# A two-layer decoder trunk: where the planes of h's second block lie, which raw buffer comes when, and where the FFN's combining stands

## The chip, the cores and the metric

The kernel runs on one core of a Trainium2 chip. The metric is the time of one execution on the device in microseconds (us), lower is better. Engines are named as in the profile: PE multiplies matrices, ACT (ScalarE) and DVE (VectorE) work on elements, POOL is GpSimd, and SP issues nearly all DMAs, in the order of its queue.

## The reference

Two layers over a residual stream of 256 tokens and 2048 features, in float32. Each layer normalises, runs a mixer (layer 0: window attention beside an mLSTM; layer 1: forgetting attention), projects its output and adds it to the stream; then it normalises again and runs a SwiGLU FFN with 5632 hidden features. A final norm follows. The FFN, around whose start the change lies:

```python
h = rms_norm(x, norm_ffn)
x = x + (silu(h @ w_gate) * (h @ w_up)) @ w_down
```

## The kernel before

**Products.** Every float32 operand is split into a high part (fp32r, a cast on ACT) and a low part (the difference, on DVE). A product of two operands is three matmuls: high x high, high x low, low x high (L244 to L246 in `gemm`, L557 to L559 in `three`). Weights arrive raw from DRAM, 256 rows x 512 columns (512 KB) at a time, by `load_raw` (L145, queue SP); L206 and L380 are casts, L207 and L381 the differences. A split weight lies in a slot of the pool `wp` (six of them, tag `hi`) or, in the FFN, in one of five such slots (`stock`) or two `triples` (tiles hi0/lo0 and hi1/lo1, 512 columns x 3).

**The FFN.** 11 groups of 512 hidden features per layer for gate and up, in three parts (`PARTS`), each part followed by two down groups. A group is one call of `pair_group`: it walks the 16 row blocks of the activation in eight pairs, in the order of a table. Kind 0 is a plain pair: its two weights are split by L206/L207 and take eight block products of three matmuls. Kind 1 is a *mixed* pair, here also *seven-product pair*: seven such products instead of eight, with weights that are sums and differences of raw blocks (L645, L648, L649 on DVE, done in the raw buffer, then L380/L381).

```python
ORDER = ((0, 0), (1, 1), (0, 2), (1, 3), (0, 4), (1, 5), (0, 6), (0, 7))
```

A mixed pair's raw weights (gate's half, then up's) go to one of three buffers taken in turn (`quads`): two tiles of the FFN's pool with the tag `quad`, and `own`, a slot of `wp`, which the projection ahead of the FFN still uses. The four mixed products (`prods`) of a group add up over its mixed pairs. `combine` merges them into the tile `c` (one buffer): a copy on ACT (L577) and three additions on DVE (L579 to L581). Then the plain sums are added (L696), silu and the gate follow (L698, L700), and the result is turned by DMA for the down groups (L729, L731, joined L736).

**The planes of h.** The projection ahead of the FFN (`out_proj`) finishes the stream h in four blocks n = 0 to 3 of 512 features. Each is turned for use as the FFN's left operand: ACT copies its halves to planes (L338), SP issues four DMA transposes (L340), and later a step called join copies the turned planes together (L345) and splits them into xh and xl (L386 on ACT, L387 on DVE, sums L326 and L294 to L297). `scrap` says where a block's planes lie meanwhile: n = 0 and 2 in the tile `c`, n = 3 in the tiles sd0/sd1, n = 1 in a quad buffer. Pairs 0 and 1 of a group need block 0, pairs 2 and 3 block 1, 4 and 5 block 2, 6 and 7 block 3.

**What sets the order.** The code emits instructions in program order; a scheduler then orders each engine's instructions by its own estimate of when their inputs and buffers are ready, earlier emitted first. So both a buffer and the place of emission move instructions on every engine.

Of the kernel before, what the change touches and what calls it, by code (L numbers as in the profile page):

```python
# [7 lines left out]
F32 = mybir.dt.float32  # L8
BF16 = mybir.dt.bfloat16
F32R = mybir.dt.float32r  # L10
# [7 lines left out]
P = 128  # L18
# [5 lines left out]
NB = 512  # L24
CK = 2
# [29 lines left out]
QUADS = 2  # L55
# [20 lines left out]
def trunk(  # L76
# [27 lines left out]
    stock, triples, quads = [], [], []  # L104
# [262 lines left out]
    def scrap(fp, n):  # L367
        if n % 2 == 0:
            box = fp.tile([P, 4, NB], F32, tag="c", name="box", bufs=1)
            halves = box[:, 0:2, :], box[:, 2:4, :]  # L370
        elif n == 3:
            halves = [fp.tile([P, 3, NB], F32, tag=f"sd{i}", name="box", bufs=1)[:, 0:CK, :] for i in range(2)]
        else:
            box = fp.tile([P, 2 * CK, NB], F32, tag="quad", name="box", bufs=QUADS)
            halves = box[:, 0:2, :], box[:, 2:4, :]
        flat, turned = (a.rearrange("p a n -> p (a n)") for a in halves)
        return flat, turned.bitcast(U16).rearrange("p (b k t q) -> p b k t q", b=2, t=NT, q=P)

# [182 lines left out]
    def pair_group(fp, par, lhs, sums, mats, order, todo=(), halves=None, inner=None, raws=None):  # L561
        plain = [two_banks(par, "acc") for _ in range(2)]
        begun = set()

        def fresh(*at):
            known = at in begun
            begun.add(at)
            return not known

        todo = list(todo)  # L570
        prods = None
        kinds = [kind for kind, _ in order]
        t0, t1 = slice(0, P), slice(P, 2 * P)

        def combine(prods):
            c = fp.tile([P, 4, NB], F32, tag="c", name="c", bufs=1)
            nc.scalar.copy(c[:, 0, :], prods[0])  # L577
            if halves is None:
                nc.vector.tensor_tensor(out=c[:, 1, :], in0=prods[3], in1=c[:, 0, :], op=ALU.add)  # L579
                nc.vector.tensor_tensor(out=c[:, 2, :], in0=prods[2], in1=c[:, 1, :], op=ALU.add)  # L580
                nc.vector.tensor_tensor(  # L581
                    out=c[:, 1:4:2, :],
                    in0=prods[1].rearrange("p (a n) -> p a n", a=1).broadcast_to([P, 2, NB]),
                    in1=c[:, 1:3, :],
                    op=ALU.add,
                )
                return c
            nc.vector.tensor_tensor(out=c[:, 2, :], in0=prods[3], in1=c[:, 0, :], op=ALU.add)
            nc.vector.tensor_tensor(out=c[:, 1, :], in0=prods[2], in1=c[:, 2, :], op=ALU.add)
            nc.vector.tensor_tensor(out=c[:, 3, :], in0=prods[1], in1=c[:, 1, :], op=ALU.add)  # L590
            nc.vector.tensor_tensor(out=c[:, 2, :], in0=prods[1], in1=c[:, 2, :], op=ALU.add)
            return c

        for pos, (kind, pair) in enumerate(order):
            k0 = 2 * pair
            if inner is not None and pos == len(order) - 1:
                c = combine(prods)
                inner()
            if not kind:
                last = pos == len(order) - 1  # L600
                walk = [(i, t) for i in range(CK) for t in range(NT)]
                if last:
                    walk.sort(key=lambda it: it[1])
                for m, (w, c0) in enumerate(mats):
                    hi, lo = load_chunk(w, k0, c0, NB)
                    run_due(todo, pos)
                    for i, t in walk:
                        ah, al = lhs(k0 + i)
                        ts = slice(t * P, (t + 1) * P)
                        three(  # L610
                            plain[m][t], ah[:, ts], al[:, ts], hi[:, i, :], lo[:, i, :],
                            fresh(m, t), last and i == CK - 1,
                        )
                continue
            first, last = 1 not in kinds[:pos], 1 not in kinds[pos + 1 :]
            if first:
                if 1 - par and halves:
                    prods = [pm.tile([P, NB], F32, tag="pm", name="prod") for _ in range(4)]
                else:
                    prods = two_banks(1 - par, "prod") + two_banks(1 - par, "prod")  # L620
            if halves:
                ra, rb = (load_raw(w, k0, c0, NB, fp, W_RAWS, raws) for w, c0 in mats)
                hg, lg = split_chunk(ra, NB)
                run_due(todo, pos)
                hu, lu = (m[:, 0, :] for m in slot())
                split_plain(hu, lu, rb[:, 0, :])
                nc.vector.tensor_tensor(out=ra[:, 1, :], in0=rb[:, 1, :], in1=ra[:, 1, :], op=ALU.subtract)
                nc.vector.tensor_tensor(out=rb[:, 1, :], in0=rb[:, 1, :], in1=rb[:, 0, :], op=ALU.subtract)
                nc.vector.tensor_tensor(out=rb[:, 0, :], in0=rb[:, 0, :], in1=ra[:, 1, :], op=ALU.subtract)
                nc.vector.tensor_tensor(out=ra[:, 0, :], in0=ra[:, 0, :], in1=rb[:, 0, :], op=ALU.subtract)  # L630
                parts = []
                for src in (ra, rb):
                    hs, ls = halves.pop(0)
                    halves.append((hs, ls))
                    split_plain(hs, ls, src)
                    parts += [(hs[:, b, :], ls[:, b, :]) for b in range(CK)]
            else:
                raw = quad()
                for m, (w, c0) in enumerate(mats):
                    load_raw(w, k0, c0, NB, into=raw[:, CK * m : CK * (m + 1), :])  # L640
                hg, lg = triple()
                latest[0] = split_plain(hg, lg, raw[:, 0:3, :])
                hu, lu = hg[:, 2, :], lg[:, 2, :]
                run_due(todo, pos)
                nc.vector.tensor_tensor(  # L645
                    out=raw[:, 1:4:2, :], in0=raw[:, 3:4, :].broadcast_to([P, 2, NB]), in1=raw[:, 1:3, :], op=ALU.subtract
                )
                nc.vector.tensor_tensor(out=raw[:, 2, :], in0=raw[:, 2, :], in1=raw[:, 1, :], op=ALU.subtract)  # L648
                nc.vector.tensor_tensor(out=raw[:, 0, :], in0=raw[:, 0, :], in1=raw[:, 2, :], op=ALU.subtract)  # L649
                (h1, l1), (h0, l0) = slot(), slot()  # L650
                split_plain(h1, l1, raw[:, 1:4:2, :])
                split_plain(h0, l0, raw[:, 0:3:2, :])
                parts = [((h0, h1)[b % 2][:, b // 2, :], (l0, l1)[b % 2][:, b // 2, :]) for b in range(4)]
            sh, sl = sums(pair)
            xa, la = lhs(k0)
            xb, lb = lhs(k0 + 1)
            three(prods[0], xb[:, t0], lb[:, t0], hg[:, 1, :], lg[:, 1, :], first, last)
            three(plain[0][0], xa[:, t0], la[:, t0], hg[:, 0, :], lg[:, 0, :], fresh(0, 0), False)
            three(plain[1][0], sh[3], sl[3], hu, lu, fresh(1, 0), False)
            three(prods[1], sh[0], sl[0], *parts[1], first, last)  # L660
            three(prods[2], sh[2], sl[2], *parts[3], first, last)
            three(prods[3], sh[1], sl[1], *parts[2], first, last)
            three(plain[0][1], xa[:, t1], la[:, t1], *parts[0], fresh(0, 1), False)
        if inner is None:
            c = combine(prods)
        return plain, c

# [128 lines left out]
    def close_layer(layer, w_out, idx, key, **rest):  # L796
        with tc.tile_pool(name=f"fp{layer}", bufs=2) as fp:
# [4 lines left out]
            x4 = fp.tile([P, 2, P], F32R, name="x4", bufs=1)  # L802
            todo = out_proj(w_out, idx, key, (*sx, x4, fp))
            sd = [fp.tile([P, nd, 4, P], F32R, tag=f"sd{i}", name=f"sd{i}", bufs=1) for i in range(2)]
            triples.extend([fp.tile([P, 3, NB], F32R, name=f"{a}{i}", bufs=1) for a in ("hi", "lo")] for i in range(2))
            stock.extend([slot() for _ in range(5)])
            own = wp.tile([P, 2, CK, NB], F32R, tag="hi", name="raw").rearrange("p a k n -> p (a k) n").bitcast(F32)
            quads.extend(fp.tile([P, 2 * CK, NB], F32, tag="quad", name="raw", bufs=QUADS) for _ in range(QUADS))
            quads.insert(1, own)
            ffn(layer, fp, sx, x4, sd, key, todo, **rest)  # L810
            stock.clear()
            triples.clear()
# [4 lines left out]
    hi, lo = slot()  # L817
# [17 lines left out]
    with tc.tile_pool(name="ev", bufs=1) as ev:  # L835
# [225 lines left out]
        with tc.tile_pool(name="mp", bufs=1) as mp:  # L1061
# [8 lines left out]
            halves = spare_halves()  # L1070
# [11 lines left out]
            c = pair_even(OFF_QM, OFF_KM, MIXQ, [(G3_AT, gates_3)])  # L1082
# [111 lines left out]
    with tc.tile_pool(name="od", bufs=1) as od:  # L1194
# [70 lines left out]
        halves = spare_halves()  # L1265
# [152 lines left out]
```

## Time and profile before

| | |
|---|---|
| median of 3 runs | 2090.94 us (2088.95 to 2092.37) |
| profiled execution | 2090.14 us |
| its span, first to last instruction | 2088.4 us |
| granted TensorE clock, mean | 0.998 |
| PE / DVE / ACT / POOL busy | 2071.4 / 1806.3 / 1367.1 / 44.0 us |
| DMA queue of SP, share of 16 engines | 65.1% |

A row of a timeline gives start (us from the span's start), duration, engine, line, operation, the tile written and those read, the shape, and in square brackets the idle time ahead of it with what ended it. A row of a table by stretches gives the stretch, its length, the busy time of PE, PEld, DVE, ACT and POOL with the count of instructions (x), the granted clock, the DMA engines' share and GB/s. A row of a group gives busy time, mean ns of one, and the idle time before them. Steps of layer 0's FFN begin near 300 us, those of layer 1's near 1365 us.

### The profile page before, as it was taken

What the parts mean: (1) busy time and instruction counts of PE and PEld (TensorE: products, weight loads), DVE (VectorE), ACT (ScalarE), POOL (GpSimd) and SP (SyncE); (2) the same over time, 40 slices, a digit from 0 to 9 for tenths busy, and PEclk for the clock granted to TensorE, in tenths of its full rate; (3) what the DMA queues carried; (4) which work ended last, traced back from release to release, by engine and by line L of the source; (5) the groups of instructions that cost most, each with busy time, mean ns of one, the idle gap of its engine ahead of it and who ended that gap; (6) DMA issues with size and microseconds to landing.
All of it is one profiled execution on the core that took longest, in us unless ns stands there. A gap on an engine that the chain in (4) does not pass through costs nothing.

```text
span 2088.4 us, 26470 instructions
## 1 busy us (share of the span) xinstructions
PE 2071.4 (99%) x9473; PEld 1714.7 (82%) x9473; DVE 1806.3 (86%) x2169; ACT 1367.1 (65%) x1649; POOL 44.0 (2%) x69
## 2 busy tenths in 40 slices
PE   9999999999999999999999999999999999999998
PEld 7878887888888888888888888877888888888887
DVE  6788768989999989998899688679989999999984
ACT  6777677665577646667677676587655667556763
POOL 1010000000000000000000001000000000000000
PEclk9999999999999999999999999999999999999999
DMA  8566577765677666665676776585756766666754
GB/s 292 174 207 194 188 242 215 222 200 198 205 221 224 210 194 224 217 209 184 203 202 218 225 200 185 155 269 188 250 188 196 233 196 217 226 205 200 235 158 159
DMA packets 309572, 434.84 MB, mean 208 GB/s; under 512 B 106413, under 2 KB 114625, under 8 KB 309313
## 3 DMA queue, kind: packets, MB, share of 16 engines
q1 hardware_dynamic: 307088, 426.27, 65.1%
q0 software_dynamic: 1632, 5.80, 0.9%
q8 instruction: 74, 1.21, 0.2%
q10 hardware_dynamic: 720, 1.09, 0.2%
q14 instruction: 58, 0.47, 0.1%
HBM read 408.68 MB, written 2.12 MB: 197 GB/s over the span
## 4 chain that ended last, share of the span: by engine, by line
PE 89%; ACT 4%; DVE 3%; DMA 2%; issue 2%; SPq 0%; POOL 0%; POOLq 0%; ACTq 0%; DVEq 0%
PE acc L558 20%; PE acc L559 20%; PE acc L557 20%; PE prod L558 5%; PE prod L557 5%; PE prod L559 5%; PE acc L245 4%; PE acc L244 4%; PE acc L246 4%; DVE hi L207 1%; ACT box L345 1%; PE p L411 1%; ACT hi L206 1%; ACT hi L380 1%; DMA raw<-in_w_gate_dram 1%
## 5 line engine op out<-in xcount | busy, mean ns | idle before, releaser
L206 ACT CAST hi<-raw 128x1024 fp32r<-128x1024 f32 (+3 forms) x561 | 567.1, 1023 | 366.5 <-PE acc L559 179.4
L207 DVE TENSOR_TENSOR hi<-raw,hi 128x1024 fp32r<-128x1024 f32 (+3 forms) x561 | 657.9, 1186 | 137.2 <-ACT hi L206 134.7
L559 PE MATMUL acc<-hi,xl 128*128 128x512 f32 x1320 | 511.9, 389 | 0.0
L557 PE MATMUL acc<-hi,xh 128*128 128x512 f32 x1320 | 495.9, 390 | 0.8 <-ACT xh L386 0.6
L380 ACT CAST hi<-raw 128x1024 fp32r<-128x1024 f32 (+2 forms) x299 | 344.9, 1168 | 225.8 <-PE acc L559 192.7
L558 PE MATMUL acc<-hi,xh 128*128 128x512 f32 x1254 | 488.0, 390 | 0.2 <-DVE hi L207 0.2
L557 PEld LDWEIGHTS acc<-hi,xh 128*128 128x128 f32 x1320 | 247.6, 188 | 53.5 <-ACT xh L386 1.8
L559 PEld LDWEIGHTS acc<-hi,xl 128*128 128x128 f32 x1320 | 248.0, 188 | 51.5
L558 PEld LDWEIGHTS acc<-hi,xh 128*128 128x128 f32 x1254 | 235.4, 188 | 50.0 <-DVE hi L207 1.0
L381 DVE TENSOR_TENSOR hi<-raw,hi 128x1024 fp32r<-128x1024 f32 (+1 forms) x204 | 240.2, 1180 | 11.1 <-ACT hi L380 10.4
L381 DVE TENSOR_TENSOR lo<-raw,hi 128x1536 fp32r<-128x1536 f32 x95 | 166.6, 1754 | 43.6 <-ACT hi L380 40.0
L559 PE MATMUL acc<-hi,ml 128*128 128x512 f32 x466 | 181.0, 389 | 0.0
L557 PE MATMUL acc<-hi,mh 128*128 128x512 f32 x466 | 173.3, 389 | 0.0
L558 PE MATMUL acc<-hi,mh 128*128 128x512 f32 x437 | 170.3, 390 | 0.4 <-DVE hi L207 0.4
L245 PE MATMUL acc<-hi,mh 128*128 128x512 f32 (+1 forms) x322 | 126.3, 392 | 0.0
L244 PE MATMUL acc<-hi,mh 128*128 128x512 f32 (+1 forms) x322 | 125.8, 391 | 0.0
L246 PE MATMUL acc<-hi,ml 128*128 128x512 f32 (+1 forms) x322 | 123.7, 391 | 0.0
L645 DVE TENSOR_TENSOR raw<-raw 128x1024 f32<-128x1024 f32 x95 | 115.5, 1217 | 0.4
L557 PEld LDWEIGHTS acc<-hi,mh 128*128 128x128 f32 x466 | 87.5, 188 | 18.6 <-ACT hi L206 0.4
L559 PEld LDWEIGHTS acc<-hi,ml 128*128 128x128 f32 x466 | 87.5, 188 | 18.1
L245 PE MATMUL acc<-hi,xh 128*128 128x512 f32 (+3 forms) x288 | 99.8, 347 | 0.2 <-DVE hi L207 0.2
L246 PE MATMUL acc<-hi,xl 128*128 128x512 f32 (+3 forms) x288 | 99.1, 345 | 0.0
(364 smaller groups left out, 3073.9 us busy)
## 6 DMA issues: line engine op xcount, KB each, us to landing
raw<-in_w_gate_dram SPq DMA_DIRECT2D x176, 512.0 KB, 4.3
raw<-in_w_up_dram SPq DMA_DIRECT2D x176, 512.0 KB, 4.8
raw<-in_w_down_dram SPq DMA_DIRECT2D x176, 512.0 KB, 4.8
raw<-in_w_in_odd_dram SPq DMA_DIRECT2D x88, 512.0 KB, 5.2
raw<-in_w_in_even_dram SPq DMA_DIRECT2D x51, 512.0 KB, 5.0
raw<-in_w_out_even_dram SPq DMA_DIRECT2D x32, 512.0 KB, 5.3
raw<-in_w_out_odd_dram SPq DMA_DIRECT2D x32, 512.0 KB, 4.7
hr<-in_w_in_even_dram SPq DMA_DIRECT2D x12, 512.0 KB, 4.4
```

The source lines that it names most:

```text
L206: latest[0] = nc.scalar.copy(hi[:, k, 0:n], raw[:, k, 0:n])
L207: nc.vector.tensor_tensor(out=lo[:, k, 0:n], in0=raw[:, k, 0:n], in1=hi[:, k, 0:n].bitcast(F32), op=ALU.subtract)
L244: nc.tensor.matmul(o, ah[:, ts], hi, start=(k == 0), stop=False)
L245: nc.tensor.matmul(o, ah[:, ts], lo, start=False, stop=False)
L246: nc.tensor.matmul(o, al[:, ts], hi, start=False, stop=(k == k_all - 1 and cs.stop == n))
L345: nc.scalar.copy(ju[:, :, b], turned[:, b, :, :, :].rearrange("p k t q -> p (k t q)"))
L380: cast = nc.scalar.copy(dst_h, src)
L381: nc.vector.tensor_tensor(out=dst_l, in0=src, in1=dst_h.bitcast(F32), op=ALU.subtract)
L557: nc.tensor.matmul(o, ah, hi, start=start, stop=False)
L558: nc.tensor.matmul(o, ah, lo, start=False, stop=False)
L559: nc.tensor.matmul(o, al, hi, start=False, stop=stop)
L645: nc.vector.tensor_tensor(out=raw[:, 1:4:2, :], in0=raw[:, 3:4, :].broadcast_to([P, 2, NB]), in1=raw[:, 1:3, :], op=ALU.subtract)
```

## The change

Three edits; each engine executes as many instructions as before.

1. The planes of block n = 1 lie in the tiles hi1/lo1, the second triple, and not in a quad buffer. The triples get explicit tags for that.
2. In gate/up and down groups (`halves is None`) `combine` is emitted right behind the last mixed pair of the table, ahead of the plain pairs that follow it, and not at the group's end.
3. `own` is the third of the three raw buffers, not the second.

```diff
@@ scrap @@
         else:
-            box = fp.tile([P, 2 * CK, NB], F32, tag="quad", name="box", bufs=QUADS)
-            halves = box[:, 0:2, :], box[:, 2:4, :]
+            halves = [fp.tile([P, 3, NB], F32, tag=f"{a}1", name="box", bufs=1)[:, 0:CK, :] for a in ("hi", "lo")]
@@ pair_group @@
         for pos, (kind, pair) in enumerate(order):
             k0 = 2 * pair
+            if 1 not in kinds[pos:] and 1 in kinds[pos - 1 : pos] and halves is None:
+                c = combine(prods)
...
-        if inner is None:
+        if inner is None and halves is not None:
             c = combine(prods)
@@ close_layer @@
-            triples.extend([fp.tile([P, 3, NB], F32R, name=f"{a}{i}", bufs=1) for a in ("hi", "lo")] for i in range(2))
+            triples.extend([fp.tile([P, 3, NB], F32R, tag=f"{a}{i}", name=f"{a}{i}", bufs=1) for a in ("hi", "lo")] for i in range(2))
...
-            quads.insert(1, own)
+            quads.append(own)
```

Lines from L375 to L595 are one lower in the changed kernel (L380 is L379, L577 is L576, L579 is L578), later ones one higher (L645 is L646).

The queue of SP, layer 0, from the end of out_proj into the FFN, before. Here raw_2993 is the first mixed pair's buffer, raw_2992 is `own` with the second pair, raw_2994 holds the third; box_2922 are the planes of block 2, box_2970 those of block 3:

```order
L145 DMA raw_2869<-in_w_out_even_dram 128x2x512
L145 DMA raw_2993<-in_w_gate_dram 128x2x512
L145 DMA raw_2993<-in_w_up_dram 128x2x512
...
L145 DMA raw_2994<-in_w_gate_dram 128x2x512
L145 DMA raw_2994<-in_w_up_dram 128x2x512
...
L340 DMA_TRANSPOSE box_2922<-box_2922 128x4x128 x4
L145 DMA raw_2992<-in_w_gate_dram 128x2x512
L340 DMA_TRANSPOSE box_2970<-box_2969 128x4x128 x4
L145 DMA raw_2992<-in_w_up_dram 128x2x512
```

The same queue in the changed kernel, where raw_2994 is the first mixed pair's buffer, raw_2995 the second's and raw_2993 (`own`) the third's; box_2579 and box_2647 are blocks 0 and 1, box_2923 and box_2970 blocks 2 and 3:

```order
L145 DMA raw_2994<-in_w_gate_dram 128x2x512
...
L145 DMA raw_2994<-in_w_up_dram 128x2x512
...
L145 DMA raw_2995<-in_w_gate_dram 128x2x512
L145 DMA raw_2995<-in_w_up_dram 128x2x512
...
L340 DMA_TRANSPOSE box_2579<-box_2579 128x4x128 x4
L340 DMA_TRANSPOSE box_2648<-box_2647 128x4x128 x4
L145 DMA raw_2782<-in_w_out_even_dram 128x2x512
...
L340 DMA_TRANSPOSE box_2923<-box_2923 128x4x128 x4
L340 DMA_TRANSPOSE box_2971<-box_2970 128x4x128 x4
L145 DMA raw_2993<-in_w_gate_dram 128x2x512
L145 DMA raw_2993<-in_w_up_dram 128x2x512
```

The first two mixed pairs' loads have moved ahead of the transposes of blocks 0 and 1, the loads into `own` behind those of blocks 2 and 3, and the chunk raw_2782 of out_proj, which stood ahead of the eight transposes of blocks 0 and 1, stands behind them.

ACT at the start of layer 0's FFN, before (hi1_2985 is the second mixed pair's split out of `own`):

```order
L206 CAST hi_2987<-raw_3088 128x1024
L380 CAST hi0_2983<-raw_2994 128x1536
L345 COPY box_2969<-box_2970 128x1024 x2
L206 CAST hi_2990<-raw_3156 128x1024
L380 CAST hi1_2985<-raw_2992 128x1536
L345 COPY box_2922<-box_2922 128x1024 x2
L386 ACTIVATE xh_58<-box_2969,gT_93 128x256 x4
L206 CAST hi_2991<-raw_3172 128x1024
L386 ACTIVATE xh_58<-box_2922,gT_93 128x256 x4
```

The same place in the changed kernel:

```order
L206 CAST hi_2988<-raw_3089 128x1024
L345 COPY box_2923<-box_2923 128x1024 x2
L379 CAST hi_2989<-raw_2995 128x1024
L385 ACTIVATE xh_58<-box_2923,gT_93 128x256 x4
L326 ACTIVATE full_3119<-box_2923,gT_93 128x256 x2
L379 CAST hi_2990<-raw_2995 128x1024
L206 CAST hi_2991<-raw_3157 128x1024
L379 CAST hi0_2984<-raw_2993 128x1536
L345 COPY box_2970<-box_2971 128x1024 x2
```

Block 2 is joined ahead of block 3, the second mixed pair's first cast is gone from here (it stands ahead, in out_proj), and what is cast from `own` is the third pair.

DVE where the second gate/up group of layer 0 combines, before (raw_3627 and raw_3643 are already the next group's first plain pair, prod_3366 is a mixed sum):

```order
L645 TENSOR_TENSOR raw_2992<-raw_2992 128x2x512
L207 TENSOR_TENSOR hi_2989<-raw_3627,hi_2989 128x1024
L207 TENSOR_TENSOR hi_2990<-raw_3643,hi_2990 128x1024
L381 TENSOR_TENSOR sd1_2982<-s4_3535,sd0_2981 128x512
L648 TENSOR_TENSOR raw_2992<-raw_2992 128x512
L579 TENSOR_TENSOR c_3602<-prod_3366,c_3602 128x512
```

The same place in the changed kernel, where those weights are raw_3628 and raw_3644 and the sum is prod_3367:

```order
L207 TENSOR_TENSOR hi_2990<-raw_3628,hi_2990 128x1024
L646 TENSOR_TENSOR raw_2995<-raw_2995 128x2x512
L578 TENSOR_TENSOR c_3528<-prod_3367,c_3528 128x512
L380 TENSOR_TENSOR sd1_2983<-s4_3541,sd0_2982 128x512
L207 TENSOR_TENSOR hi_2991<-raw_3644,hi_2991 128x1024
L649 TENSOR_TENSOR raw_2995<-raw_2995 128x512
```

The first addition of the combining has moved ahead of one split of the next group, one smaller difference and one step of the next mixed pair's weights. It stands behind the splits of its own group's last plain pairs in both.

## The prediction

> **What bounds the kernel now.** I read the page's parts 1 and 2 first, then the busy time by stretches of 20 us, then TensorE's list of waits, and last the timeline of the places where PE loses.
>
> ```profile
> span 2088.4 us, 26470 instructions
> PE 2071.4 (99%) x9473; PEld 1714.7 (82%) x9473; DVE 1806.3 (86%) x2169; ACT 1367.1 (65%) x1649; POOL 44.0 (2%) x69
> ```
>
> PE is the bound almost throughout, so an edit that moves other engines' work gains only where PE waits. The table by stretches says where (the number behind PE's busy time counts matmuls):
>
> ```profile
> 280.00:300.00 20.00, 20.00 (x90) 16.54 (x90) 10.75 (x16) 16.47 (x25) 0.00 (x0) 1.00 0.72 206
> ...
> 340.00:360.00 20.00, 16.37 (x61) 11.91 (x62) 19.82 (x27) 18.61 (x26) 0.00 (x0) 0.91 0.48 157
> 360.00:380.00 20.00, 20.00 (x90) 16.56 (x89) 20.00 (x27) 12.16 (x13) 0.00 (x0) 1.00 0.75 256
> 380.00:400.00 20.00, 20.00 (x90) 16.54 (x89) 19.38 (x21) 15.94 (x17) 0.00 (x0) 1.00 0.62 183
> 400.00:420.00 20.00, 20.00 (x90) 16.57 (x89) 19.86 (x24) 10.71 (x12) 0.00 (x0) 1.00 0.86 290
> 480.00:500.00 20.00, 19.77 (x87) 16.25 (x87) 19.48 (x21) 6.78 (x7) 0.00 (x0) 1.00 0.76 260
> 1540.00:1560.00 20.00, 19.83 (x86) 15.99 (x86) 19.84 (x23) 7.22 (x8) 0.00 (x0) 1.00 0.77 262
> ```
>
> A full stretch has 90 matmuls, 20/90 = 0.222 us each. Two stretches, drawn around the losses, show what is missing at the head of each layer's FFN:
>
> ```profile
> 338.90:355.60 16.70, 12.21 (x44) 8.28 (x43) 15.64 (x23) 16.29 (x23) 0.00 (x0) 0.90 0.43 148
> 1404.00:1424.00 20.00, 17.99 (x71) 12.38 (x70) 19.41 (x30) 17.85 (x27) 0.00 (x0) 1.00 0.45 142
> ```
>
> Layer 0: 44 x 0.222 = 9.8 us of work in 16.7 us, 6.9 us lost. Layer 1: 71 x 0.222 = 15.8 us in 20, 4.2 us lost. The down groups' first stretches (x87, x86) lack 3 and 4 matmuls, 0.7 and 0.9 us. That is 12.7 us in all, and the bound of any gain here. The waits in layer 0, on the timelines of PE, ACT and SP:
>
> ```profile
> 341.17 0.50 PE L557 MATMUL prod<-hi,xh 128*128 128x512 f32 x1 [2.03 <-ACT hi L380]
> ...
> 342.96 0.80 PE L558 MATMUL prod<-lo,xh 128*128 128x512 f32 x1 [0.83 <-DVE lo L381]
> ...
> 346.53 0.50 PE L557 MATMUL acc<-hi,xh 128*128 128x512 f32 x1 [0.64 <-ACT xh L386]
> ...
> 355.40 0.50 PE L558 MATMUL prod<-hi,sx 128*128 128x512 f32 x1 [0.99 <-DVE hi L381]
> ```
>
> ```profile
> 336.28 2.56 ACT L345 COPY box<-box 128x1024 uint16<-128x1024 uint16 x2 [3.99 <-DMA box<-box]
> ...
> 339.64 1.47 ACT L380 CAST hi<-raw 128x1536 fp32r<-128x1536 f32 x1
> 341.01 2.55 ACT L345 COPY box<-box 128x1024 uint16<-128x1024 uint16 x2
> 343.43 1.70 ACT L386 ACTIVATE xh<-box,gT 128x256 fp32r<-128x256 f32 x4
> ```
>
> ```profile
> 329.18 0.53 SPq L145 DMA_DIRECT2D raw<-in_w_gate_dram  x1
> 329.80 5.14 SPq L340 DMA_TRANSPOSE box<-box  x4
> 335.00 0.58 SPq L145 DMA_DIRECT2D raw<-in_w_up_dram  x1
> ```
>
> The second seven-product pair's weights go to `own`, a slot of the wp pool that out-proj keeps until 329.18; their second half is issued at 335.00, behind the four transposes of block n=3; the cast of it (L380, 339.64) stands on ACT behind that block's join, and PE stops for it until 341.17. Next it lacks the lows (342.96), then block n=2's planes, joined at 341.01 only (346.53).
>
> **The change, part by part.** I name lines as in the kernel before.
>
> *Buffers (edits one and three).* With `own` as the third quad, pairs one and two both have quad buffers that are free early, since n=1's planes now lie in the second triple. In the order all four of their loads stand before the transposes of n=0 and n=1; pair two is cast and split during out-proj, and `own` takes pair three, behind the transposes of n=2 and n=3. On ACT the join of n=2 comes ahead of that of n=3. Nothing is added: each engine has as many instructions as before. What leaves 340 to 360 is pair two's splitting, by these groups:
>
> ```profile
> L381 DVE TENSOR_TENSOR lo<-raw,hi 128x1536 fp32r<-128x1536 f32 x95 | 166.6, 1754 | 43.6 <-ACT hi L380 40.0
> ...
> L645 DVE TENSOR_TENSOR raw<-raw 128x1024 f32<-128x1024 f32 x95 | 115.5, 1217 | 0.4
> ...
> L381 DVE TENSOR_TENSOR hi<-raw,hi 128x1024 fp32r<-128x1024 f32 (+1 forms) x204 | 240.2, 1180 | 11.1 <-ACT hi L380 10.4
> ...
> L649 DVE TENSOR_TENSOR raw<-raw 128x512 f32<-128x512 f32 x95 | 64.8, 682 | 0.1
> L648 DVE TENSOR_TENSOR raw<-raw 128x512 f32<-128x512 f32 x95 | 64.7, 682 | 0.2
> ```
>
> On DVE that is 1.75 + 1.22 + 0.68 + 0.68 + 2 x 1.18 = 6.7 us. The part that goes to 280 to 300, where DVE is busy 10.75 of 20 us, is hidden by idle time there. Without that cover the 6.7 us would come back as lateness in out-proj.
>
> Layer 0's first pause: its cast is done some 40 us early, so 2.03 + 0.83 us go, and with them the slow matmuls that follow (clock below). n=2's last transposes stand before the gate load of 329.18, so its join can run from about 331 on ACT; 2.56 us of join and 1.70 us of L386 bring its planes by about 335 to 336, and the 0.64 us at 346.53 goes too. Pair three's second half is issued at about 335.6 and lands some 5 us later (before, the half issued at 335.00 was being cast at 339.64), so its cast is done by about 342. In the new order PE reaches that pair 45 matmuls behind the place of the pause (338.97 + 45 x 0.227 = 349.2). Neither takes the pause's place.
>
> The limit is DVE. From 340 to 420 it is busy 19.82 + 20.00 + 19.38 + 19.86 = 79.1 us of 80. Take 6.7 us out; PE running 6.9 us earlier pulls as much later work in: 79.3 us of 80. It just fits on average, not at every instruction: walking the new order through these durations, the pieces of pair three come up to 1.4 us late around 352 to 356. I leave 1.4 us, a gain of 5.5 us; the ends are 3 us (half of the loss returns later) and 6.9.
>
> Layer 1 loses in smaller pieces, the largest of them here:
>
> ```profile
> 1397.71 1.48 ACT L380 CAST hi<-raw 128x1536 fp32r<-128x1536 f32 x1 [2.31 <-DMA raw<-in_w_up_dram]
> ...
> 1406.66 0.50 PE L557 MATMUL prod<-hi,xh 128*128 128x512 f32 x1 [0.69 <-ACT xh L386]
> 1410.94 0.72 PE L557 MATMUL prod<-hi,sx 128*128 128x512 f32 x2 [0.66 <-ACT hi L380]
> 1420.00:1440.00 20.00, 20.00 (x89) 16.12 (x88) 20.00 (x26) 12.00 (x13) 0.00 (x0) 1.00 0.76 259
> ```
>
> The 2.31 us of idle ACT and the 1.48 us cast behind it go, so the joins that follow start up to 3.8 us earlier and both pauses shrink. But DVE is busy all 20 us of the next stretch, and in my walk one split near 1431 comes some 1.7 us late. I take a gain of 2.0 of the 4.2 us, with ends at 0 and 4.2.
>
> *One queue pays.* One out-proj chunk, raw_2782 and its counterpart in layer 1, is now issued behind the eight transposes of n=0 and n=1. The place it takes is that of the chunk behind them before:
>
> ```profile
> 296.27 1.05 ACT L206 CAST hi<-raw 128x1024 fp32r<-128x1024 f32 x1 [1.89 <-DMA raw<-in_w_out_even_dram]
> 297.35 1.23 DVE L207 TENSOR_TENSOR hi<-raw,hi 128x1024 fp32r<-128x1024 f32 x1 [2.87 <-ACT hi L206]
> 299.54 0.39 PE L244 MATMUL acc<-hi,mh 128*128 128x512 f32 x1
> ```
>
> Its lows would be there at 298.6; PE wants them at about 299.5. The margin is 0.9 us, and not smaller in layer 1. I book nothing, with +2 us per layer as the worse end (a transfer that lands some 3 us late) and no gain possible, since PE runs without a gap there.
>
> *The combining.* In the order of gate/up groups its first DVE instruction (L579) moves ahead of one split L207 (of the next group's first pair), one L648 and one L381, and no further: `c` is a single tile, held until the group before has been joined from it.
>
> ```profile
> 407.66 2.35 DVE L207 TENSOR_TENSOR hi<-raw,hi 128x1024 fp32r<-128x1024 f32 x2
> ...
> 413.80 0.39 PE L558 MATMUL acc<-hi,xh 128*128 128x512 f32 x1
> ...
> L581 DVE TENSOR_TENSOR c<-prod,c 128x1024 f32<-128x1024 f32 x33 | 40.0, 1214 | 0.0
> ...
> L579 DVE TENSOR_TENSOR c<-prod,c 128x512 f32<-128x512 f32 x33 | 22.5, 681 | 1.8 <-PE prod L559 1.8
> ```
>
> PE at 413.80 reads what the first of the two splits wrote, which was done at 407.66 + 1.22 = 408.88: a lead of 4.9 us, one typical for the body. A delay of 0.68 us, even of the whole combining (0.68, as much for L580, and 1.21: 2.6 us), stays below that. A gain cannot come of it either where all 90 matmuls of a stretch are there already. I take 0, with ends at -1.6 us (the down groups' two starts) and +8 us (the rival below).
>
> The sum: -5.5 - 2.0 + 0 + 0 = -7.5 us. The profiled run took 2090.14 us, 1.7 us of it outside the span; it lies 0.8 us below the median, so 2082.6 on its scale is 2083.4 against the median; I say 2083.5.
>
> *The clock.* Layer 0's pauses were followed by a low clock; layer 1's, none above 0.7 us of idle PE, by none:
>
> ```profile
> 343.00:346.50 3.50, 2.89 (x6) 0.53 0.32 123
> ```
>
> At 0.53 for 3.5 us this costs about 1.6 us, already inside the 6.9. No stop of that length should be left, so the sum has no term for it; if the late chunk of out-proj stopped PE for 2 us, as the pause at 341 did, 1.6 us would come on top. [...]
>
> **The rivals.**
>
> *No change (0.22).* DVE becomes the bound: 79.3 of 80 us is an average, and if the work pulled in queues behind pair three's lows, PE stops at 352 and again up to 380 for what it gained. For it: DVE at 20.00 from 360 to 380. Against it: PE waits nowhere there now, with the same DVE share. Layer 0 then keeps a gain of 3 us and layer 1 none: 2090.9 - 3 = 2088.
>
> *Slower (0.18): the combining ahead of splits.* L577 on ACT and L579 on DVE now stand ahead of a split that PE needs next, and both wait for PE's last product of the seven-product pairs. An engine that gets there before PE has finished stands, and the splits queued behind it with it. It decides where that wait, the combining and the split itself pass the lead of 4.9 us: with 1.8 us, the one wait that L579's row has now, 1.8 + 2.6 + 1.2 = 5.6, 0.7 us too late. In each of the 22 gate/up groups (11 per layer) that is +15 us, less 7.5 at the heads: 2098.5; in half of them, 2091. Against it: L579 waits once in 33 now, and in the order it has passed one split only.
>
> *The change does not do what it says (0.02).* For the loads the order excludes it. For the combining it nearly holds, and then the time is the forecast's.
>
> **How the numbers follow.** The forecast (0.58) covers 2079 to 2086.5: all 11.1 us of the heads gone, or 4.5 us only. No change covers 2087 to 2092. The range of 2079 to 2095 takes in both and the part of the slower rival that strikes some groups only, or two late chunks (+3.6 us each) with the heads' gain lost. A measurement of this kernel tells 0.2%, 4.2 us, from no change. Faster by more than that: the forecast with a little of the second case, 0.60; slower by more: 0.18; within: 0.22.
>
> **What would show it.** Right: 338.9 to 355.6 with some 69 matmuls instead of 44 and no clock below 1.00; the L380 cast of pair two before 300; 1404 to 1424 with 80 or more; all stretches of 20 us from 360 on still at 90. Wrong: TensorE's waits showing L246 or L245 behind L206 near 299 (the late chunk); new waits of L558 on DVE L207 or L381 in every group, and L579's wait on PE grown from 1.8 us to tens of us (the slower rival); or waits of the old size, moved from 341 to 352 and later (no change).

## The result, and the profile after

The changed kernel takes 2082.85 us in the median (2082.55 to 2084.5, 6 runs), the kernel before 2091.88 us (2088.95 to 2093.99, 6 runs). The medians lie 9.0 us apart. The ratio is 0.9959, with a 95% interval of 0.9949 to 0.9969, which is 6.5 to 10.7 us less and clear of the 0.2% that could be told from no change.

The page of the changed kernel, its span and its engines:

```profile
span 2080.8 us, 26492 instructions
PE 2068.0 (99%) x9473; PEld 1715.3 (82%) x9473; DVE 1806.2 (87%) x2169; ACT 1368.0 (66%) x1649; POOL 43.2 (2%) x69
```

DVE, ACT and POOL are as busy as before to 1 us. PE stands 4.2 us less (span less busy time: 17.0 us before, 12.8 now), and its busy time fell by 3.4 us for the same 9473 matmuls. The old losses had both: from 338.9 to 355.6 PE stood, and was also booked busy for 12.21 us with 44 matmuls that take 9.8 at 0.222 us each. The table by stretches of the changed kernel, with the two stretches around the old losses (44 and 71 matmuls before):

```profile
260.00:280.00 20.00, 18.70 (x87) 15.05 (x85) 13.27 (x17) 11.05 (x17) 0.69 (x1) 1.00 0.88 309
338.90:355.60 16.70, 16.42 (x73) 13.28 (x72) 14.60 (x21) 15.08 (x21) 0.00 (x0) 1.00 0.72 267
1404.00:1424.00 20.00, 19.68 (x86) 15.68 (x85) 20.00 (x28) 16.12 (x21) 0.00 (x0) 1.00 0.64 206
1420.00:1440.00 20.00, 19.34 (x86) 15.70 (x85) 20.00 (x24) 10.43 (x10) 0.00 (x0) 1.00 0.73 238
```

Layer 0's stretch now holds 73 matmuls at a clock of 1.00. Layer 1's holds 86, but the stretch behind it has lost three. And 260 to 280, where nothing was lost before, has 87 instead of 93: a new loss. Before, this stretch read:

```profile
260.00:280.00 20.00, 20.00 (x93) 16.48 (x92) 13.27 (x19) 11.76 (x19) 0.69 (x1) 1.00 0.67 230
```

TensorE's list of waits in the changed kernel names the new loss:

```profile
PE acc L557 <- DVE hi L207: 1.8, 5, 0.7
PE acc L244 <- DVE h L394: 1.4, 1, 1.4
```

The waits for ACT's L380 and L386 and DVE's L381 are gone. What is left in the FFNs are five short waits for splits (L207), three of them at the FFN's heads and two at down groups; new is one of 1.4 us in out-proj, for the additions to h.

To see where the time went, I put the n-th matrix instruction of PE in one trace beside the n-th in the other (start in us; both kernels have 9473). A negative difference means that the changed kernel is ahead:

```
n       before   changed  difference  what lies between this row and the one above
850      155.1     153.8     -1.3     first mixer: the code is the same
1380     272.1     270.8     -1.3     out-proj up to there
1450     288.0     288.4     +0.5     the new wait, +1.7
1650     333.3     333.8     +0.5     out-proj's end, FFN's start
1850     385.9     380.1     -5.8     head of layer 0's FFN, -6.2
6500    1403.7    1398.6     -5.1     the rest of layer 0, layer 1's mixer, +0.6
6700    1453.3    1445.7     -7.6     head of layer 1's FFN, -2.4
9472    2080.4    2072.8     -7.6     all the rest, 0.0
```

The two heads bring 8.6 us, out-proj takes 1.7 back, and the rest of the FFNs and layer 1's mixer are as they were to 0.6 us. The 1.3 us ahead of n = 850 lie in code that the change doesn't touch, so this much differs between two executions.

Layer 0's head on ACT, changed kernel: the join of block 2 (L345) first, then pair three's cast out of `own`, then the join of block 3:

```profile
330.91 2.56 ACT L345 COPY box<-box 128x1024 uint16<-128x1024 uint16 x2
...
340.52 1.48 ACT L379 CAST hi<-raw 128x1536 fp32r<-128x1536 f32 x1 [1.84 <-DMA raw<-in_w_up_dram]
341.91 2.56 ACT L345 COPY box<-box 128x1024 uint16<-128x1024 uint16 x2
```

Block 2 is joined at 330.91, not at 341.01, and the cast that waits for a late load ends at 342.00, some 7 us ahead of the 349.2 us at which PE was expected at that pair.

The new wait, on the timelines of SP, ACT, DVE and PE of the changed kernel, in this order:

```profile
267.88 0.47 SPq L145 DMA_DIRECT2D raw<-in_w_up_dram  x1
```

```profile
274.95 1.48 ACT L379 CAST hi<-raw 128x1536 fp32r<-128x1536 f32 x1 [3.32 <-DMA raw<-in_w_up_dram]
```

```profile
276.46 1.76 DVE L380 TENSOR_TENSOR lo<-raw,hi 128x1536 fp32r<-128x1536 f32 x1 [3.58 <-ACT hi L379]
278.26 1.23 DVE L646 TENSOR_TENSOR raw<-raw 128x1024 f32<-128x1024 f32 x1
279.40 1.28 DVE L394 TENSOR_TENSOR h<-acc,h 128x512 f32<-128x512 f32 x2
```

```profile
280.14 0.50 PE L244 MATMUL acc<-hi,mh 128*128 128x512 f32 x1 [1.44 <-DVE h L394]
```

The first mixed pair's second half was issued at 267.88 and was there 7 us later, DMA engines being busy to 0.88 in that stretch. DVE stood 3.58 us for the cast of it and then did two of that pair's steps, while the additions of block 0 to h were queued behind. They free the sums' PSUM banks, and PE needed those. Before, the same additions (there L395) waited for PE's sums alone and began 2.8 us sooner:

```profile
276.62 1.29 DVE L395 TENSOR_TENSOR h<-acc,h 128x512 f32<-128x512 f32 x2 [2.45 <-PE acc L246]
```

### The profile page after: what moved, and what is told of

Same layout as the page of the kernel before. It is cut to its first block, busy times and chain, and to the rows that moved or that the text cites. A ratio compares the mean times of both kernels' runs of the same rounds, so it can differ in the third digit from the quotient of the medians.

```text
span 2080.8 us, 26492 instructions
## 1 busy us (share of the span) xinstructions
PE 2068.0 (99%) x9473; PEld 1715.3 (82%) x9473; DVE 1806.2 (87%) x2169; ACT 1368.0 (66%) x1649; POOL 43.2 (2%) x69
## 4 chain that ended last, share of the span: by engine, by line
PE 87%; DVE 5%; ACT 3%; DMA 2%; issue 2%; SPq 0%; POOL 0%; POOLq 0%; ACTq 0%; DVEq 0%
PE acc L557 20%; PE acc L558 20%; PE acc L556 20%; PE prod L556 5%; PE prod L557 5%; PE prod L558 5%; PE acc L245 4%; PE acc L244 4%; PE acc L246 4%; DVE hi L207 2%; ACT box L345 1%; DMA raw<-in_w_up_dram 1%; PE p L410 1%; DMA raw<-in_w_gate_dram 1%; DMA raw<-in_w_out_even_dram 1%
## 5 line engine op out<-in xcount | busy, mean ns | idle before, releaser
L207 DVE TENSOR_TENSOR hi<-raw,hi 128x1024 fp32r<-128x1024 f32 (+3 forms) x561 | 659.8, 1188 | 115.7 <-ACT hi L206 113.8
L379 ACT CAST hi<-raw 128x1024 fp32r<-128x1024 f32 (+2 forms) x299 | 345.8, 1169 | 247.3 <-PE acc L558 195.2
L380 DVE TENSOR_TENSOR hi<-raw,hi 128x1024 fp32r<-128x1024 f32 (+1 forms) x204 | 241.1, 1183 | 18.2 <-ACT hi L379 17.8
L380 DVE TENSOR_TENSOR lo<-raw,hi 128x1536 fp32r<-128x1536 f32 x95 | 166.8, 1756 | 56.1 <-ACT hi L379 55.9
L646 DVE TENSOR_TENSOR raw<-raw 128x1024 f32<-128x1024 f32 x95 | 115.9, 1220 | 0.5
```

What stands on the lines that cost most here:

```text
L207: nc.vector.tensor_tensor(out=lo[:, k, 0:n], in0=raw[:, k, 0:n], in1=hi[:, k, 0:n].bitcast(F32), op=ALU.subtract)
L379: cast = nc.scalar.copy(dst_h, src)
L380: nc.vector.tensor_tensor(out=dst_l, in0=src, in1=dst_h.bitcast(F32), op=ALU.subtract)
L646: nc.vector.tensor_tensor(out=raw[:, 1:4:2, :], in0=raw[:, 3:4, :].broadcast_to([P, 2, NB]), in1=raw[:, 1:3, :], op=ALU.subtract)
```

## Experiments

Theory A: the time lies in the order of raw buffers and loads at the FFN's heads. Rivals: the combining gives part of it (B); what costs is the quad buffer that block 1's planes hold (C).

**1. The buffers without the combining.**

```diff
 after.py, but combine() where it was:
-            if 1 not in kinds[pos:] and 1 in kinds[pos - 1 : pos] and halves is None:
-                c = combine(prods)
-        if inner is None and halves is not None:
+        if inner is None:
             c = combine(prods)
```

> Edits one and three (buffers) with the combining where it was. Theory A (the gain is the buffers' alone): as the changed kernel, 2082 to 2084 us, 9 us below before, with PE's 1.4 us wait for the additions to h near 280 us still there. Theory B (the combining gives part): 2 us or more slower than the changed kernel, 2085 us or more, with PE waits at the starts of the down groups.

2083.74 us, ratio to before 0.9965 (0.9952 to 0.9977). Matched as above it ends 7.6 us ahead of before, as the changed kernel does, with +2.0 us in out-proj, -6.1 and -2.8 us at the heads. So the combining is not needed for the gain; its median is 0.9 us above the changed kernel's, and the two intervals overlap.

**2. The combining alone.**

```diff
 before.py:
+            if 1 not in kinds[pos:] and 1 in kinds[pos - 1 : pos] and halves is None:
+                c = combine(prods)
-        if inner is None:
+        if inner is None and halves is not None:
             c = combine(prods)
```

> Edit two (the combining) alone. Theory A: no change, 2091 to 2093 us, layer 0's stretch of 338.9 to 355.6 us still with some 44 matmuls. Theory B: 2 us or more faster than before, from the body or the down groups' starts.

2090.80 us, 0.9999 (0.9990 to 1.0008): nothing, as A had it. Its table by stretches has the old loss:

```profile
338.90:355.60 16.70, 12.44 (x43) 8.70 (x44) 16.00 (x23) 16.28 (x23) 0.00 (x0) 0.90 0.38 132
```

**3. The planes alone.**

```diff
 before.py, scrap(), and the triples' tags as in the change:
-            box = fp.tile([P, 2 * CK, NB], F32, tag="quad", name="box", bufs=QUADS)
-            halves = box[:, 0:2, :], box[:, 2:4, :]
+            halves = [fp.tile([P, 3, NB], F32, tag=f"{a}1", name="box", bufs=1)[:, 0:CK, :] for a in ("hi", "lo")]
```

> Edit one alone (planes of block n=1 in the second triple, the wp slot still second of the raw buffers). Theory A (what costs is that the second pair's weights wait for the wp slot): layer 0's pause at 341 us stays, and the early split of the first pair adds its 1.7 us wait near 280 us: 2092 to 2094 us. Theory C (what costs is the quad buffer that the planes hold): most of the 9 us gained, 2083 to 2086 us.

2090.30 us, 0.9995 (0.9986 to 1.0003): no change that can be told, but not for the reason that A gave. Two effects cancel. In out-proj it loses 4.3 us, at layer 0's head it gains 3.7 (the pause of 2.03 us is gone there: both halves of the second pair are now issued ahead of block 3's transposes, at 331.44 and 332.01 with the transposes at 332.58), and at layer 1's head it gains nothing. The loss in out-proj, on PE and in the table by stretches:

```profile
282.63 0.79 PE L244 MATMUL acc<-hi,mh 128*128 128x512 f32 x1 [2.69 <-DVE h L394]
```

```profile
282.50:285.50 3.00, 2.87 (x7) 0.50 0.06 23
```

It is the wait of the changed kernel, here of 2.69 us, and followed by a granted clock of 0.50.

**4. The wp slot third, alone.**

```diff
 before.py, close_layer():
-            quads.insert(1, own)
+            quads.append(own)
```

> Edit three alone (the wp slot third of the raw buffers, planes of n=1 still in a quad buffer). Theory A: the pause at 341 us goes without the planes' move, and so without the early split and its 1.7 us wait near 280 us: 2081 to 2083 us, 1 to 2 us below the changed kernel. Theory C: the second pair's loads come only behind the transposes of n=0 and n=1, its split crowds ACT and DVE at the FFN's start, and half of the loss stays: 2086 to 2089 us.

2086.29 us, 0.9976 (0.9967 to 0.9985): 5 us faster, half of the changed kernel's gain. Neither theory fits. A was right at the heads: by the matched instructions -6.2 us (layer 0) and -3.5 us (layer 1), nothing lost in out-proj. C's total came out, but not from where C had it: the loss comes later, 3.3 us from 385 to 530 us and 3.1 us from 1453 to 1566. PE, then DVE, in this kernel:

```profile
410.81 0.50 PE L557 MATMUL acc<-hi,xh 128*128 128x512 f32 x1 [1.26 <-DVE c L579]
...
469.06 0.50 PE L557 MATMUL acc<-hi,mh 128*128 128x512 f32 x1 [0.77 <-ACT mh L380]
472.13 0.51 PE L557 MATMUL acc<-hi,mh 128*128 128x512 f32 x1 [0.46 <-ACT hi L380]
```

```profile
409.47 0.69 DVE L649 TENSOR_TENSOR raw<-raw 128x512 f32<-128x512 f32 x1
410.07 0.69 DVE L579 TENSOR_TENSOR c<-prod,c 128x512 f32<-128x512 f32 x1
```

The new order of buffers moved the queues of later groups too: the combining came so late that PE waited for the PSUM bank that it frees (a group's plain sums take the banks of the last group's mixed products), and at the first down group ACT does two raw casts ahead of the cast that PE waits for (the timeline of ACT):

```profile
465.69 2.85 ACT L380 CAST hi<-raw 128x1536 fp32r<-128x1536 f32 x2
468.43 1.06 ACT L380 CAST mh<-pf 128x512 fp32r<-128x512 f32 x2
```

**5. The wp slot third and the combining early, planes as before.**

```diff
 experiment 4, with experiment 2's lines
```

> Edits two and three, planes of n=1 left in a quad buffer. Edit three alone lost no time at the FFN's heads, but got new PE waits: 1.3 us for L579 at 411 us (the combining too late) and 0.8 + 0.5 us at each start of layer 0's and 1's first down groups (the turn's cast L380 behind two raw casts). Theory D (edit two is there for these waits): emitted earlier, the combining stands two rows ahead on DVE and the wait at 411 us goes; with it some 2 us: 2083 to 2085 us. If the down groups' waits go too, 2080 to 2082 us. Theory E (edit two moves too little): 2086 to 2087 us as with edit three alone.

2083.65 us, 0.9964 (0.9950 to 0.9977): theory D. TensorE's waits in this kernel:

```profile
PE acc L557 <- ACT mh L380: 1.4, 2, 0.7
PE acc L557 <- ACT hi L380: 0.9, 2, 0.5
PE acc L557 <- DVE c L579: 0.2, 1, 0.2
```

PE's wait for L579 fell from 2.6 us in two (experiment 4) to 0.2; the down groups' waits stayed. So the combining's place, worth nothing in the orders of before and after, is worth some 2.6 us (2086.29 to 2083.65; 2.9 by the matched instructions) where another order had made it late. The two ratios' intervals overlap a little; the waits that went are what shows it.

**6. The changed kernel, with the additions first.**

```diff
 after.py (add_out returns its last addition; held gets that of block 0):
-                latest[0] = split_plain(hg, lg, raw[:, 0:3, :])
+                with tc.issue_after(held.pop().ins) if held else ExitStack():
+                    latest[0] = split_plain(hg, lg, raw[:, 0:3, :])
```

> The changed kernel with the first mixed pair's low split (L380) queued on DVE behind the additions of block n=0 to h, for layer 0 and layer 1. If the 1.4 us PE wait near 280 us comes from that split standing ahead of the additions, the wait goes, PE's stretch of 260 to 280 us has 90 matmuls again, and the time is 1.7 us below the changed kernel: 2081 to 2082 us. If the additions are late for another reason (the load traffic that the early loads bring), it stays: 2083 us.

2080.53 us (2080.16 to 2081.26), 0.9949 (0.9936 to 0.9961): the lowest median of all, 2.3 us below the changed kernel's. The two ratios' intervals overlap, but by the matched instructions it ends 9.9 us ahead of before, the changed kernel 7.6. Its DVE (L395 is L394 of the changed kernel) and its stretches:

```profile
276.36 1.29 DVE L395 TENSOR_TENSOR h<-acc,h 128x512 f32<-128x512 f32 x2 [2.45 <-PE acc L247]
278.25 1.76 DVE L381 TENSOR_TENSOR lo<-raw,hi 128x1536 fp32r<-128x1536 f32 x1 [0.60 <-ACT hi L380]
```

```profile
260.00:280.00 20.00, 20.00 (x93) 16.48 (x92) 12.83 (x17) 11.86 (x17) 0.69 (x1) 1.00 0.86 305
1404.00:1424.00 20.00, 20.00 (x89) 16.09 (x88) 20.00 (x27) 14.85 (x20) 0.00 (x0) 1.00 0.70 242
1420.00:1440.00 20.00, 20.00 (x90) 16.57 (x89) 20.00 (x23) 12.96 (x13) 0.00 (x0) 1.00 0.64 210
```

The additions now wait for PE and not for the split, the 93 matmuls are back with the same load traffic (0.86), and layer 0's +1.7 us is gone (0.0 there by the matched instructions). The order was the cause. Layer 1's head gained too, -4.0 us instead of -2.4, which was not expected and is why the time fell below the range: the scheduler's order there changed along, and the two waits for L207 of the changed kernel (0.32 us at 1415, 0.67 at 1426) are gone though DVE is just as full. Which of the moved rows did it was not tried.

## Why the prediction was right, and where not

**The bound and the place** were right. The heads gave the gain, and no run gained more than the 12.7 us.

**Layer 0's head**: forecast -5.5 us with 69 matmuls in the stretch, measured -6.2 with 73. Block 2's join and pair three's cast came where the steps put them (331, 342). The second pair's cast did not: it was to run before 300, some 40 us early, and ran at 310.10, still 29 us ahead of its old place and in time. The 1.4 us left for pieces of pair three was too much: what PE lost there is a wait of 0.28 us at 354.63 and some tenths to 385 (360 to 380 has 88 matmuls, not the 90 that were forecast).

**Layer 1's head**: forecast -2.0, measured -2.4, with the forecast late split, for which PE waits 0.67 us at 1426:

```profile
1426.11 0.50 PE L557 MATMUL acc<-hi,xh 128*128 128x512 f32 x1 [0.67 <-DVE hi L207]
```

**The step that failed** is the cover: that the second pair's splitting goes to 280 to 300 and "is hidden by idle time there". None of it came there. With edit one, the tiles hi1/lo1 into which that pair is split hold block 1's planes, and DVE read them for xl until 308.74 (first row below); the pair's cast follows at 310.10 (second row), and its pieces on DVE lie between 311 and 339, where PE lost nothing.

```profile
307.07 1.67 DVE L386 SCALAR_TENSOR_TENSOR xl<-box,gT,xh 128x256 fp32r<-128x256 f32 x4
310.10 1.48 ACT L379 CAST hi<-raw 128x1536 fp32r<-128x1536 f32 x1
```

What moved ahead into the middle of out-proj is the *first* pair's split, for which the sum has no term. Its loads were issued at 293 before and at 266 to 268 now, and its cast went from 305.94 to 274.95. DVE had idle time there too (busy 13.27 of 20 us from 260 to 280), but the split ran there at 276.46, behind 3.58 us in which DVE stood for its cast, ahead of additions that PE needed (279.40). That cost 1.7 us, where the sum had 0. The row of the first pair's cast before:

```profile
305.94 1.47 ACT L380 CAST hi<-raw 128x1536 fp32r<-128x1536 f32 x1
```

The queue that the prediction did watch, SP's, was not the one that paid: the late chunk was cast at 296.91, its lows followed at 298.00, and PE did not wait for them.

```profile
296.91 1.05 ACT L206 CAST hi<-raw 128x1024 fp32r<-128x1024 f32 x1 [1.23 <-DMA raw<-in_w_out_even_dram]
```

**The combining**: 0 forecast, 0 measured (experiments 1 and 2). The slower rival did not happen; L578's wait for PE is 1.8 us in all, once, as L579's was. The reverse, a combining that is late, did, in experiment 4. DVE as the new bound could hold only for layer 1, and for about 2 us there; in experiment 6 most of these are gone too with DVE just as full, so they were a matter of order.

**The sum**: -6.2 - 2.4 + 1.7 + 0.6 = -6.3 us by these two traces, -7.6 with the start's 1.3 us, -9.0 us by the medians; -7.5 was said. The errors of the terms partly cancelled, and that -7.6 lies so near to -7.5 is luck. Before's profiled run lies 1.7 us below its median over six runs, the changed kernel's 0.3 us: that is the difference between -7.6 and -9.0. Why before spreads over 5 us and the changed kernel over 2 has to do with the clock, in part: of 36 further runs of before, the four with a granted clock of 0.999 took 2090.0 us in the mean, the eight with 0.996 or less 2092.2. The rest stays open.

## What to carry to other kernels

When an engine's work is moved to a stretch where the engine idles, look at what is queued behind the moved instruction there and when its own input arrives: here DVE stood 3.58 us for a cast with additions behind it that PE needed, and PE waited 1.44 us for them, so the idle time did not hide the work. And list everything that a freed buffer lets start earlier, not only the work that you meant to move: here the first pair moved as well. A buffer's turn in a ring is an order of loads: the buffer that comes free last should take the work that is needed last. And where a scheduler places everything, an edit at one end moves queues more than 100 us away, so each edit is worth something only beside the others: the wp slot's turn alone gave half, with either of the other two nearly all.

## What the runs showed of the hardware

The granted clock was low behind some pauses of PE and 1.00 behind others. Before had pauses of 2.03 us up to 341.17 and of 0.83 us up to 342.96, and a clock of 0.53 from 343.00 to 346.50 (the prediction's rows). Experiment 3 had one of 2.69 us up to 282.63, and 0.50 from 282.50 to 285.50 (its rows stand there). Experiment 2 had one of 2.02 us up to 340.81, and then:

```profile
340.81 0.73 PE L557 MATMUL prod<-hi,xh 128*128 128x512 f32 x1 [2.02 <-ACT hi L380]
342.60 0.79 PE L558 MATMUL prod<-lo,xh 128*128 128x512 f32 x1 [0.21 <-DVE lo L381]
340.80:342.60 1.80, 1.59 (x3) 0.53 0.98 312
342.60:345.90 3.30, 2.44 (x6) 0.74 0.29 107
```

Behind the 1.71 us of experiment 1 (first two rows) and the 1.44 us of the changed kernel's new wait (third row) the clock was 1.00:

```profile
280.87 0.50 PE L244 MATMUL acc<-hi,mh 128*128 128x512 f32 x1 [1.71 <-DVE h L394]
280.00:284.00 4.00, 3.13 (x14) 1.00 0.21 70
280.00:284.00 4.00, 3.86 (x17) 1.00 0.22 53
```

These five cases stand for themselves: what decides whether the clock falls was not shown.

The price: the six matmuls behind the pause of experiment 3 take 2.73 us (282.63 to 285.36), not 6 x 0.227 = 1.36, at the pace of the changed kernel at a clock of 1.00 (ten in 2.27 us, 276.04 to 278.31). By these rows that pause of 2.69 us cost, by estimate, some 1.4 us on top of itself; the prediction took 1.6 us on top of a stop of 2 us, from before's row.
